# Two-layer encoder trunk on one core: weight sums by accumulating DMAs, and an instruction order from a timeline simulation

## The chip, the cores and the metric

One core of a Trainium2 chip runs the kernel: TensorE (PE) with its weight loads (PEld), VectorE (DVE), ScalarE (ACT), GpSimd (POOL) and SyncE (SP), whose queue issues nearly all DMAs. The metric is the time of one execution in microseconds (us).

## The reference

Two request batches, a prompt of 512 tokens and a sample of 256, go through two layers with shared weights (D = 1024, feed-forward width 2816). The kernel treats them as one block of 768 tokens.

```
x <- LN1(alpha*x + W_out [DiffAttn_ALiBi(x) ; BiMLSTM(x)])
x <- LN2(alpha*x + ConvGatedFFN(x))

s = einsum('bqhcd,bshcd->bhcqs', qi, k)           # 4 heads, 2 score maps each
p = softmax(s + bias, axis=-1)
a = p[:, :, 0] - lam * p[:, :, 1]
out = einsum('bhqs,bshd->bqhd', a, v)
```

Beside the four attention heads stand four heads of a two-directional mLSTM in chunks of 128 tokens. The feed-forward part multiplies by a gate matrix and an up matrix, runs a convolution of width 3 over the gate, and multiplies the result into the down matrix.

## The kernel before

**Arithmetic.** Each product is made in three matmul passes (PASSES) of operands split into a high part and a low part. `Weights` brings a weight piece of 128x512 in by an SP DMA (`_load`, six raw buffers, names raw0, raw1, ...) and converts it (`_conv`): ACT writes the high part wh (L171), DVE the low part wl (L172). Twelve slots hold converted pieces until PE has used them.

**Attention stage.** PE works through generators that `weave` mixes by fixed priorities. Per head, sequence and query block (the digits in a name: s2231 is head 2, sequence from token tile 2 on, block 3, map 1) the chain is: scores s on PE (L728, L729), tp on DVE (L730), two exponentials on ACT (L734), the difference of the maps in tp on DVE (L737), aT on PE (L740), a copy of aT, u on PE (L744), ao on DVE (L752, after a power on POOL), aoT on PE (L757). The mLSTM chunk c has qkT, kq and num on PE and pt, qet, den and hq on DVE (num20 is chunk 2, pair 0). Matmuls that depend on little stand between them as filling: lo (L345, one of the dense projections), and aqkA and aqkB (L355), the q and k projections of the next head, which DVE and ACT then split into sQ, sK and kL. Behind head 3 comes the output projection wo (L898).

**Feed-forward stage.** For each of 22 feature tiles of 128 per layer, `ff_tile` makes gate and up by a seven-product scheme (`product`, p1 to p7, L942) that needs four sums of weight pieces, T1 to T4. Two of them run on POOL and two on DVE (L149), on raw pieces, before conversion. After three tiles (four for one group) `down` runs 12 chunks dn (L1002), whose results DVE adds to acc (L1009). The pair of lines that makes a sum is in `Weights._value`.

**Order.** The program's instructions go to each engine in the order that the tile framework's scheduler gives them by their priorities. Each engine then runs its own list strictly in order.

Of the kernel before, what the change touches and what calls it, by code (L numbers as in the profile page):

```python
# [13 lines left out]
F32 = mybir.dt.float32  # L14
# [7 lines left out]
T = SA + SB  # L22
# [73 lines left out]
class Weights:  # L96

    def __init__(self, nc, raw_pool, hl_pool, prio):  # L100
        self.nc, self.raw_pool, self.hl_pool, self.prio = nc, raw_pool, hl_pool, prio
        self.dram, self.blocks = [], []
        self.uses, self.raw, self.hl = {}, {}, {}
        self.n_dma = self.n_conv = self.n_got = self.n_done = 0
        self.diff_pool = None
        self.urgency = PR_CONV

# [6 lines left out]

    def block(self, src, n, dst=None):
        self.blocks.append((src, n, dst))
        for j in self._pieces(src):
            self.uses[j] += 1
# [6 lines left out]
    def _pieces(self, src):  # L125

        if not isinstance(src, dict):
            return [src]
        if src.get("planned"):
            return []  # L130
        src["planned"] = True
        return self._pieces(src["a"]) + self._pieces(src["b"])


    def _load(self):

        while self.n_dma < len(self.dram) and (self.n_dma < NRAW or self.uses[self.n_dma - NRAW] == 0):
            ap, n = self.dram[self.n_dma]
            t = self.raw_pool.tile([128, WCOL], F32, tag="raw", name=f"raw{self.n_dma}")[:, :n]
            self.nc.sync.dma_start(t, ap)  # L140
            self.raw[self.n_dma] = t
            self.n_dma += 1

    def _value(self, src, n):
        if isinstance(src, dict):
            if "tile" not in src:
                a, b = self._value(src["a"], n), self._value(src["b"], n)
                src["tile"] = self.diff_pool.tile([128, 512], F32, tag=src["tag"], name=f"{src['tag']}_{self.n_conv}")
                src["engine"].tensor_tensor(out=src["tile"], in0=a, in1=b, op=ALU.subtract)  # L149
                for x in (src["a"], src["b"]):  # L150
                    if not isinstance(x, dict):
                        self.uses[x] -= 1
            return src["tile"]
        return self.raw[src]

    def _conv(self, i):
        src, n, dst = self.blocks[i]
        self._load()
        v = self._value(src, n)
        if callable(dst):  # L160
# [45 lines left out]
def trunk(ctx, nc, tc, d, o, depth=DEPTH):  # L206
# [59 lines left out]
    for l in range(depth):  # L266
        if l:
            for u in range(4):
                W.unit(d["w_c1"][l, u], 1056)
        for u in range(4):  # L270
            W.unit(d["w_av"][l, u])
        for h in range(4):
            W.unit(d["w_aq"][l, h])
            W.unit(d["w_ak"][l, h])
            if h == 0 or h == (1 if L1 else 2):
                for u in range(4):
                    W.unit(d["w_lv" if h == 0 else "w_lo"][l, u])
        for hf in range(2):
            for u in range(4):
                W.unit(d["w_out"][l, hf, u])  # L280
        early = {}
        for i in range(FF_EARLY):
            early[i] = [W.piece(d["w_g"][l, i, :, p * 512:(p + 1) * 512], 512) for p in range(2)]
            for src in early[i]:
                W.block(src, 512)
        for kind, i in ffn_seq:
            if kind == "f":

                def half(w, p):
                    return W.piece(d[w][l, i, :, p * 512:(p + 1) * 512], 512)  # L290

                if i in early:
                    g0, g1 = early[i]
                else:
                    g0, g1 = half("w_g", 0), None
                u0, u1 = half("w_u", 0), half("w_u", 1)
                if g1 is None:
                    g1 = half("w_g", 1)
                t1 = {"a": u0, "b": g0, "tag": "T1", "engine": G}
                t2 = {"a": u1, "b": t1, "tag": "T2", "engine": V}  # L300
                t3 = {"a": u1, "b": u0, "tag": "T3", "engine": G}
                t4 = {"a": t2, "b": g1, "tag": "T4", "engine": V}
# [65 lines left out]
    for l in range(depth):  # L368
# [502 lines left out]
        def combine(t):  # L871

            y0, y1 = acc[:, t, 0:512], acc[:, t, 512:1024]
            if t < 3:
                todo[t] = [(A11, y0), (A12, y1)]
                return
            x0, x1 = acc[:, t - 3, 0:512], acc[:, t - 3, 512:1024]
            E = V if t in VT else G
            s1, s2, s3, s4 = (sp.tile([128, 512], F32, tag=f"S{i}", name=f"S{i}_{t}") for i in (1, 2, 3, 4))
            E.tensor_tensor(out=s1, in0=y0, in1=y1, op=ALU.add)  # L880
            E.tensor_tensor(out=s2, in0=s1, in1=x0, op=ALU.subtract)
            E.tensor_tensor(out=s3, in0=x0, in1=y0, op=ALU.subtract)
# [62 lines left out]
        def ff_tile(f):  # L945
# [21 lines left out]
            V.scalar_tensor_tensor(out=g[:, hi_], in0=p4, scalar=-1.0, in1=u3, op0=ALU.mult, op1=ALU.add)  # L967
            p5 = bank(f"p5_{f}")
            product(p5, S1)
            V.tensor_tensor(out=u4, in0=p5, in1=u2, op=ALU.add)  # L970
            V.tensor_tensor(out=up[:, hi_], in0=p5, in1=u3, op=ALU.add)
# [128 lines left out]
def build(arrays, depth=DEPTH):  # L1100
# [18 lines left out]
```

## Time and profile before

| | us |
|---|---|
| median of three runs (1812.57 to 1816.02) | 1815.83 |
| the profiled execution | 1814.85 |
| its span, first to last instruction | 1813.1 |
| PE busy | 1772.2 |
| DVE busy | 1348.4 |
| ACT busy | 774.3 |
| POOL busy | 244.4 |

Busy times are sums over instructions in which neighbours may overlap: the pitch from one start to the next is shorter than a duration. The granted TensorE clock was 0.998 of full speed on average.

### The profile page before, as it was taken

What the parts mean: (1) busy time and instruction counts of PE and PEld (TensorE: products, weight loads), DVE (VectorE), ACT (ScalarE), POOL (GpSimd) and SP (SyncE); (2) the same over time, 40 slices, a digit from 0 to 9 for tenths busy, and PEclk for the clock granted to TensorE, in tenths of its full rate; (3) what the DMA queues carried; (4) which work ended last, traced back from release to release, by engine and by line L of the source; (5) the groups of instructions that cost most, each with busy time, mean ns of one, the idle gap of its engine ahead of it and who ended that gap; (6) DMA issues with size and microseconds to landing.
All of it is one profiled execution on the core that took longest, in us unless ns stands there. A gap on an engine that the chain in (4) does not pass through costs nothing. (4 is left out here: it accounts for less than half of the span.)

```text
span 1813.1 us, 26263 instructions
## 1 busy us (share of the span) xinstructions
PE 1772.2 (98%) x9692; PEld 1575.5 (87%) x9692; DVE 1348.4 (74%) x2592; ACT 774.3 (43%) x1636; POOL 244.4 (13%) x266
## 2 busy tenths in 40 slices
PE   8999999999999999999999999999999999999998
PEld 8877887889889889899898778878899898898996
DVE  4546887599877787787955468876997787787778
ACT  4445667144334334344233556671453343343340
POOL 2001011141111111110110011101411110111102
PEclk9999999999999999999999999999999999999999
DMA  5312221303122122123232123122122221221211
GB/s 190 100 53 71 76 60 59 139 24 95 57 82 82 47 82 73 56 69 96 94 97 80 53 64 94 47 86 107 37 87 70 65 82 51 78 82 47 82 65 70
DMA packets 89232, 138.09 MB, mean 76 GB/s; under 512 B 7792, under 2 KB 33008, under 8 KB 89104
## 3 DMA queue, kind: packets, MB, share of 16 engines
q1 hardware_dynamic: 88384, 136.05, 23.7%
q8 instruction: 76, 1.25, 0.3%
q14 instruction: 52, 0.43, 0.1%
q10 hardware_dynamic: 720, 0.37, 0.1%
HBM read 130.00 MB, written 6.39 MB: 75 GB/s over the span
## 5 line engine op out<-in xcount | busy, mean ns | idle before, releaser
L942 PE MATMUL p<-actA,wh 128*128 128x384 f32 x1408 | 363.5, 338 | 3.2 <-DVE g L967 3.2
L171 ACT ACTIVATE wh<-raw 128x512 fp32r<-128x512 f32 (+1 forms) x348 | 215.8, 631 | 275.3 <-PE p L942 110.1
L172 DVE TENSOR_TENSOR wl<-raw,wh 128x512 fp32r<-128x512 f32 (+1 forms) x348 | 244.0, 712 | 62.2 <-ACT wh L171 61.7
L942 PE MATMUL p<-actB,wh 128*128 128x384 f32 x1056 | 270.1, 337 | 0.0
L942 PEld LDWEIGHTS p<-actA,wh 128*128 128x128 f32 x1408 | 254.7, 188 | 5.8 <-DVE g L967 3.8
L942 PE MATMUL p<-actA,wl 128*128 128x384 f32 x704 | 237.3, 337 | 0.0
L149 POOL TENSOR_TENSOR T<-raw,raw 128x512 f32<-128x512 f32 x88 | 120.3, 1370 | 837.4 <-DVE wl L172 483.9
L1002 PE MATMUL dn<-wh,actB 128*128 128x512 f32 x576 | 209.1, 396 | 1.4 <-DVE acc L1009 1.4
L171 ACT ACTIVATE wh<-T 128x512 fp32r<-128x512 f32 x176 | 108.5, 629 | 220.6 <-DVE acc L1009 105.3
L942 PEld LDWEIGHTS p<-actB,wh 128*128 128x128 f32 x1056 | 191.2, 188 | 0.0
L1002 PE MATMUL dn<-wh,ring 128*128 128x512 f32 x480 | 179.2, 397 | 1.6 <-DVE acc L1009 1.6
L942 PE MATMUL p<-actB,wl 128*128 128x384 f32 x528 | 177.2, 336 | 0.0
L1009 DVE TENSOR_TENSOR acc<-acc,dn 128x512 f32<-128x512 f32 x144 | 98.3, 683 | 72.2 <-PE dn L1002 72.0
L172 DVE TENSOR_TENSOR wl<-T,wh 128x512 fp32r<-128x512 f32 x176 | 129.8, 749 | 22.1 <-ACT wh L171 22.0
L1002 PEld LDWEIGHTS dn<-wh,actB 128*128 128x128 f32 x576 | 108.0, 188 | 30.3 <-DVE acc L1009 3.4
L942 PEld LDWEIGHTS p<-actA,wl 128*128 128x128 f32 x704 | 132.2, 188 | 0.1
L898 PE MATMUL wo<-wh,actB 128*128 128x512 f32 x384 | 122.9, 397 | 0.0
L1002 PE MATMUL dn<-wl,actB 128*128 128x512 f32 x288 | 113.2, 393 | 0.0
L1002 PEld LDWEIGHTS dn<-wh,ring 128*128 128x128 f32 x480 | 90.0, 188 | 24.6 <-DVE acc L1009 4.2
L942 PEld LDWEIGHTS p<-actB,wl 128*128 128x128 f32 x528 | 99.1, 188 | 0.0
L1002 PE MATMUL dn<-wl,ring 128*128 128x512 f32 x240 | 94.7, 395 | 0.0
L898 PEld LDWEIGHTS wo<-wh,actB 128*128 128x128 f32 x384 | 71.8, 188 | 16.2
(270 smaller groups left out, 3387.9 us busy)
## 6 DMA issues: line engine op xcount, KB each, us to landing
raw<-in_w_g_dram SPq DMA_DIRECT2D x88, 256.0 KB, 2.8
raw<-in_w_u_dram SPq DMA_DIRECT2D x88, 256.0 KB, 2.6
raw<-in_w_down_dram SPq DMA_DIRECT2D x88, 256.0 KB, 2.7
raw<-in_w_out_dram SPq DMA_DIRECT2D x32, 256.0 KB, 2.7
pt<-scr_m SPq DMA_DIRECT2D x12, 512.0 KB, 3.9
qet<-scr_e SPq DMA_DIRECT2D x12, 512.0 KB, 5.2
raw<-in_w_c_dram SPq DMA_DIRECT2D x16, 264.0 KB, 4.0
raw<-in_w_av_dram SPq DMA_DIRECT2D x16, 256.0 KB, 3.5
```

Of the source, the lines that this page charges most:

```text
L149: src["engine"].tensor_tensor(out=src["tile"], in0=a, in1=b, op=ALU.subtract)
L171: self.nc.scalar.activation(h, v, AF.Identity)
L172: self.nc.vector.tensor_tensor(out=l, in0=v, in1=h.bitcast(F32), op=ALU.subtract)
L898: PE.matmul(p, actB[:, k, a, t * 128:(t + 1) * 128], units[k][1 + b], start=n + i == 0, stop=n == 7 and i == 2)
L942: PE.matmul(ps, blk[1 + a][:, k * 128:(k + 1) * 128], x[:, k, b, :], start=k + i == 0, stop=k == 3 and i == 2)
L1002: PE.matmul(p, x, (wh_, wl_)[b], start=k + i == 0, stop=k == nf - 1 and i == 2)
L1009: V.tensor_tensor(out=z, in0=z, in1=p, op=ALU.add)
```

## The change

**Sums by DMA.** For the first three feature tiles of each layer (N_ENG) the four sums stay on POOL and DVE. From the fourth tile on (19 tiles in each layer) a sum is one SP load into a T tile and one accumulating DMA that POOL issues onto it: T1 from DRAM, T2 from T1's tile, T3 from DRAM, T4 from T2's tile. All T tiles share a ring of four buffers (NSUM). Signs are arranged so that each sum is an addition, so the seven products are used with other signs and come in another order. Per tile eight DMAs for sums and three raw loads (2.75 MB) take the place of four raw loads (1 MB), and two POOL and two DVE instructions per tile are gone.

**Order.** The context is made with `schedule_with_timeline_sim=True`; the lists of all engines come out in another order.

```diff
@@ class Weights
+        while self.diff_pool is not None and self.n_sum < len(self.sums) and (self.n_sum < NSUM or self.sums[self.n_sum - NSUM]["read"]):
+            s = self.sums[self.n_sum]
...
+            t = self._slot(s)
+            self.nc.sync.dma_start(t, s["a"])
+            self.nc.gpsimd.dma_start(t, s["b"]["tile"] if isinstance(s["b"], dict) else s["b"], accum_op=ALU.add)
...
+    def _slot(self, s):
+        s["tile"] = t = self.diff_pool.tile([128, 512], F32, tag="T", name=f"T{self.n_sum}", bufs=NSUM)
...
-                src["engine"].tensor_tensor(out=src["tile"], in0=a, in1=b, op=ALU.subtract)
+                src["engine"].tensor_tensor(out=self._slot(src), in0=v[0], in1=v[1], op=ALU.add)
@@ the list of weight blocks
+                if i < N_ENG:
...
+                    t1 = W.sum(l, u0, g0, G)
+                    t2 = W.sum(l, u1, t1, V)
...
+                    u1 = W.piece(at("w_u", 1), 512)
+                    t1 = W.sum(l, at("w_u", 0), at("w_g", 0))
+                    t2 = W.sum(l, at("w_u", 1), t1)
+                    t3 = W.sum(l, at("w_u", 1), at("w_u", 0))
+                    t4 = W.sum(l, at("w_g", 1), t2)
-                for src in (t4, t2, t3, t1, u1) if i in early else (g0, g1, t4, t2, t3, t1, u1):
+                for src in (t1, t2, t3, t4, u1) if i in early else (g0, g1, t1, t2, t3, t4, u1):
@@ ff_tile
-            p4 = bank(f"p4_{f}")
-            product(p4, A22)
+            p5 = bank(f"p5_{f}")
+            product(p5, S1)
...
-            V.tensor_tensor(out=u2, in0=p6, in1=m1, op=ALU.add)
+            V.tensor_tensor(out=u2, in0=m1, in1=p6, op=ALU.subtract)
+            V.tensor_tensor(out=u4, in0=p5, in1=u2, op=ALU.add)
...
-    with tile.TileContext(nc) as tc:
+    with tile.TileContext(nc, schedule_with_timeline_sim=True) as tc:
```

The order is shown at three places, all in layer 0; layer 1 has the same pattern. In the rows an x at the end counts repeats, the number behind an underscore marks a tile, and line numbers of the changed kernel are 15 to 23 higher (L187 there is L172 before, L750 is L728).

**Place 1, middle of the attention stage.** PE's list behind qkT3, the transposes for mLSTM chunk 3, in the kernel before:

```order
L592 MATMUL qkT3_2180<-ident_214,hq_226 128x128 x4
L355 MATMUL aqkA21_2244<-actA_70,wh48_1456 128x512 x2
L355 MATMUL aqkA21_2244<-actA_70,wl48_1457 128x512
L728 MATMUL s2000_2353<-sK_229,sQ_228 128x256
L729 MATMUL s2000_2353<-kL_230,sQ_228 128x256
L728 MATMUL s2001_2357<-sK_229,sQ_228 128x256
L729 MATMUL s2001_2357<-kL_230,sQ_228 128x256
L345 MATMUL lo1_2478<-wh49_1462,actA_70 128x512
L345 MATMUL lo1_2478<-wl49_1463,actA_70 128x512
L345 MATMUL lo1_2478<-wh49_1462,actA_70 128x512
L345 MATMUL lo1_2478<-wh50_1468,actA_70 128x512
L345 MATMUL lo1_2478<-wl50_1469,actA_70 128x512
```

The list of PE there in the changed kernel, behind the same qkT3 and chunk 2's first products:

```order
L655 MATMUL num20_2189<-cst21_1804,qet2_2068 128x129
L658 MATMUL num20_2189<-vaug_237,pt2_2009 128x129 x2
L655 MATMUL num22_2317<-cst21_1804,qet2_2068 128x129
L658 MATMUL num22_2317<-vaug_237,pt2_2009 128x129 x2
L655 MATMUL num23_2318<-cst21_1804,qet2_2068 128x129
L658 MATMUL num23_2318<-vaug_237,pt2_2009 128x129 x2
L637 MATMUL kq3_2386<-qz_1847,kt3_2185 128x128 x4
L762 MATMUL aT200_2366<-ident_214,tp200_2350 128x128 x2
L766 MATMUL u20_2347<-av_227,aT200_2369 128x128 x2
L762 MATMUL aT201_2420<-ident_214,tp201_2404 128x128 x2
L614 MATMUL qkT4_2395<-ident_214,hq_226 128x128 x4
L750 MATMUL s2210_2590<-sK_229,sQ_228 128x512
```

The filling is gone from between. In the whole piece of the list from qkT3 to aoT22 the kernel before has 48 matmuls of lo (lo1 and lo2), 27 of aqkA and 38 of aqkB; the changed one has 24 (lo5). Those 113 now stand ahead of qkT3, and so do 72 more that stood behind aoT22 (lo3, lo4 and aqkA31).

DVE's list in the same piece, where chunk 4's den is made, before:

```order
L597 COPY qz_1847<-qkT5_2578 64x256
L730 ISA tp222_2665,mn222_2666<-s2220_2668,dneg_233 128x512
L730 ISA mn222_2666 128x1
L730 ISA tp222_2665,mn222_2666<-s2221_2672,dneg_233 128x512
L730 ISA mn222_2666 128x1
L643 SCALAR_TENSOR_TENSOR den40_2625<-num40_2615,cols_239 128x2
L643 SCALAR_TENSOR_TENSOR den41_2632<-num41_2616,cols_239 128x2
L644 TENSOR_TENSOR den40_2625<-num40_2615,den40_2625 128x2
L644 TENSOR_TENSOR den41_2632<-num41_2616,den41_2632 128x2
L645 RECIPROCAL den40_2625<-den40_2625 128x2
L682 SCALAR_TENSOR_TENSOR sg2_2718<-sgt2_2719,sg2_2718 128x512
L645 RECIPROCAL den41_2632<-den41_2632 128x2
```

And DVE's list in the changed kernel, behind the same den:

```order
L667 RECIPROCAL den41_2632<-den41_2632 128x2
L758 SCALAR_TENSOR_TENSOR cc223_2741<-sm022_2528,nlam_221,cc223_2741 128x1
L187 TENSOR_TENSOR wl65_3318<-raw65_2297,wh65_3317 128x512
L759 SCALAR_TENSOR_TENSOR tp223_2739<-tp223_2739,cc223_2741 128x512
L770 SCALAR_TENSOR_TENSOR sm022_2528<-sm022_2528 128x4
L187 TENSOR_TENSOR wl66_3324<-raw66_2303,wh66_3323 128x512
L187 TENSOR_TENSOR wl67_3330<-raw67_3297,wh67_3329 128x512
L670 SCALAR_TENSOR_TENSOR hq_226<-num40_2615,den40_2625,hq_226 128x128
L670 SCALAR_TENSOR_TENSOR hq_226<-num41_2616,den41_2632,hq_226 128x128
L187 TENSOR_TENSOR wl68_3336<-raw68_3303,wh68_3335 128x512
L187 TENSOR_TENSOR wl69_3342<-raw69_3309,wh69_3341 128x512
L704 SCALAR_TENSOR_TENSOR sg4_3201<-sgt4_3202,sg4_3201 128x512
```

Eight conversions of output weights, wl65 to wl72, have moved into this piece from behind head 3's first blocks; 256-wide pieces of aqkB3 have moved out of it. From the reading of qkT3 to ao22 the DVE list had 151 instructions (41 of 512 elements per partition, 16 of 256, 25 of 128, 69 of one to four) and has 150 (51, 8, 24, 67). SP's list in the piece also changes: the load of qet5, which DVE multiplies 12 rows further on, stands behind the raw loads 71 to 75, and raw75 uses the buffer of raw69.

**Place 2, end of the attention stage.** PE's list behind s3011, the last scores of head 3, before (lo5 goes on behind these rows for 19 more matmuls, with aoT32, u30 and aT301 between):

```order
L729 MATMUL s3011_3216<-kL_230,sQ_228 128x256
L345 MATMUL lo5_3253<-wh49_1462,actA_70 128x512
L345 MATMUL lo5_3253<-wl49_1463,actA_70 128x512
L744 MATMUL u32_2972<-av_227,aT323_3131 128x128 x4
L740 MATMUL aT300_3168<-ident_214,tp300_3152 128x128 x2
L345 MATMUL lo5_3253<-wh49_1462,actA_70 128x512
L345 MATMUL lo5_3253<-wh50_1468,actA_70 128x512
L345 MATMUL lo5_3253<-wl50_1469,actA_70 128x512
```

And in the changed kernel:

```order
L762 MATMUL aT323_3126<-ident_214,tp323_3110 128x128 x4
L766 MATMUL u32_2972<-av_227,aT323_3131 128x128 x4
L762 MATMUL aT300_3168<-ident_214,tp300_3152 128x128 x2
L762 MATMUL aT301_3225<-ident_214,tp301_3209 128x128 x2
L779 MATMUL aoT32_3143<-ident_214,ao32_3141 128x128 x4
L384 MATMUL loT5_3286<-ident_214,hq_226 128x128 x4
L766 MATMUL u30_3149<-av_227,aT300_3171 128x128 x2
L921 MATMUL wo02_3449<-wh64_3311,actB_2834 128x512
L921 MATMUL wo02_3449<-wl64_3312,actB_2834 128x512
L921 MATMUL wo02_3449<-wh64_3311,actB_2834 128x512
L766 MATMUL u30_3149<-av_227,aT301_3228 128x128 x2
L779 MATMUL aoT30_3249<-ident_214,ao30_3247 128x128 x2
```

The last scores are followed by their own transposes, the last u and the last aoT with 8 transposes and 3 matmuls of wo02 between; wo00's last three matmuls, which need the result of aoT30, come right behind, and most of wo00 and wo02 stand earlier.

**Place 3, the feed-forward stage.** PE's list at the first group of dn, before, at the passage from one chunk to the next (dn001 ends, dn002 begins):

```order
L1002 MATMUL dn001_4696<-wh106_4446,actB_2834 128x512
L1002 MATMUL dn001_4696<-wh107_4466,ring_4043 128x512
L1002 MATMUL dn001_4696<-wl107_4467,ring_4043 128x512
L1002 MATMUL dn001_4696<-wh107_4466,ring_4043 128x512
L1002 MATMUL dn002_4707<-wh105_4427,actB_2834 128x512
L1002 MATMUL dn002_4707<-wl105_4428,actB_2834 128x512
L1002 MATMUL dn002_4707<-wh105_4427,actB_2834 128x512
L1002 MATMUL dn002_4707<-wh106_4446,actB_2834 128x512
```

And in the changed kernel behind the same chunk:

```order
L1025 MATMUL dn001_4714<-wh107_4481,ring_4033 128x512
L1025 MATMUL dn001_4714<-wl107_4482,ring_4033 128x512
L1025 MATMUL dn001_4714<-wh107_4481,ring_4033 128x512
L965 MATMUL p1_4_4881<-actA_70,wh111_4580 128x384 x2
L965 MATMUL p1_4_4881<-actA_70,wl111_4581 128x384
L965 MATMUL p1_4_4881<-actA_70,wh111_4580 128x384 x2
```

Before, 12 chunks stand in a row; now products of the next feature tile come between pairs of chunks.

## Rows read from the trace of the kernel before

**Rows 1.** The page, part 1: busy us, share of the span and instructions.

```profile
PE 1772.2 (98%) x9692; PEld 1575.5 (87%) x9692; DVE 1348.4 (74%) x2592; ACT 774.3 (43%) x1636; POOL 244.4 (13%) x266
```

**Rows 2.** Windows: length, busy us (count) of PE, PEld, DVE, ACT, POOL, PEclk, DMA, GB/s.

```profile
104.40:217.00 112.60, 110.17 (x668) 89.85 (x667) 70.77 (x201) 61.42 (x178) 10.47 (x14) 1.00 0.19 57
217.00:270.10 53.10, 50.63 (x336) 44.40 (x335) 46.97 (x157) 38.78 (x126) 6.35 (x8) 1.00 0.22 65
270.10:329.90 59.80, 57.15 (x304) 46.50 (x303) 40.74 (x101) 37.07 (x95) 5.71 (x6) 1.00 0.33 118
1117.70:1171.40 53.70, 50.88 (x336) 44.15 (x335) 47.12 (x157) 38.57 (x125) 5.83 (x8) 1.00 0.22 65
452.20:870.20 418.00, 416.40 (x2161) 384.96 (x2161) 324.19 (x528) 156.98 (x255) 45.49 (x34) 1.00 0.24 74
```

**Rows 3.** Timeline of PE, layer 0: start, duration, line, operands, count.

```profile
217.00 0.60 PE L592 MATMUL qkT<-ident,hq 128*128 128x128 f32 x4
...
270.11 0.60 PE L757 MATMUL aoT<-ident,ao 128*128 128x128 f32 x4
```

**Rows 4.** Windows with the tile lo alone: PE, PEld, ACT.

```profile
217.00:270.10 53.10, 12.83 (x48) 8.66 (x48) 2.36 (x4) 1.00 0.22 65
```

**Rows 5.** Windows with the tile aqkA alone: PE, PEld, DVE, ACT.

```profile
217.00:270.10 53.10, 7.96 (x28) 4.86 (x27) 2.75 (x4) 3.49 (x6) 1.00 0.22 65
```

**Rows 6.** Windows with the tile aqkB alone: PE, PEld, DVE, ACT.

```profile
217.00:270.10 53.10, 5.79 (x38) 4.88 (x38) 1.28 (x4) 0.76 (x2) 1.00 0.22 65
```

**Rows 7.** Chain of waits, layer 1: start us, us on the chain, engine, line, count.

```profile
1219.65 45.25 PE wo L898 x195
...
1294.45 0.60 DVE S L880
...
1353.64 25.15 PE dn L1002 x108
...
1448.48 44.09 PE p L942 x252
```

**Rows 8.** Timeline of DVE in the middle of the attention stage.

```profile
221.48 0.40 DVE L730 CUSTOM_DVE_ANT_0 tp<-s,dneg 128x256 f32<-128x256 f32 x1
...
221.81 0.16 DVE L645 RECIPROCAL den<-den 128x2 f32<-128x2 f32 x1
221.89 0.40 DVE L730 CUSTOM_DVE_ANT_0 tp<-s,dneg 128x256 f32<-128x256 f32 x1
...
222.59 0.61 DVE L648 SCALAR_TENSOR_TENSOR hq<-num,den,hq 128x128 f32<-128x128 f32 x2 [0.29 <-ACT hq L647]
```

**Rows 9.** Timeline, layer 0, head 3: end of scores to tp, end of u to aoT.

```profile
287.01 0.39 PE L729 MATMUL s<-kL,sQ 128*128 128x512 f32 x1
...
290.13 0.75 DVE L737 SCALAR_TENSOR_TENSOR tp<-tp,cc 128x512 f32<-128x512 f32 x1
...
310.94 0.63 PE L744 MATMUL u<-av,aT 128*128 128x128 f32 x4
...
314.39 0.41 PE L757 MATMUL aoT<-ident,ao 128*128 128x128 f32 x2 [0.27 <-DVE ao L752]
```

**Rows 10.** The page, part 5: an ACT group, busy us and mean ns.

```profile
L171 ACT ACTIVATE wh<-raw 128x512 fp32r<-128x512 f32 (+1 forms) x348 | 215.8, 631 | 275.3 <-PE p L942 110.1
```

**Rows 11.** Waits of PE in 452.2:870.2: us in total, times, longest us.

```profile
PE dn L1002 <- DVE acc L1009: 1.6, 5, 0.6
```

**Rows 12.** Groups of DVE in 452.2:870.2, one of the two sums.

```profile
L149 DVE TENSOR_TENSOR T<-raw,T 128x512 f32<-128x512 f32 x18 | 12.3, 684 | 8.5 <-POOL T L149 8.5
```

**Rows 13.** The page, part 6: issues, KB each, median us to landing.

```profile
raw<-in_w_g_dram SPq DMA_DIRECT2D x88, 256.0 KB, 2.8
...
qet<-scr_e SPq DMA_DIRECT2D x12, 512.0 KB, 5.2
```

**Rows 14.** Windows at the end of the span, columns as in rows 2.

```profile
1804.00:1808.00 4.00, 0.96 (x5) 0.43 (x3) 2.92 (x8) 0.54 (x1) 3.21 (x3) 0.91 0.05 17
1808.00:1813.00 5.00, 0.00 (x0) 0.00 (x0) 1.63 (x5) 0.51 (x1) 1.15 (x2) 0.50 0.54 196
```

More of the change, by code (lines that the diff above doesn't have):

```diff
@@ L86 @@
 NSG = 3
+NSUM = 4
+N_ENG = 3
 AT1 = 11
@@ L103, in __init__ @@
         self.uses, self.raw, self.hl = {}, {}, {}
-        self.n_dma = self.n_conv = self.n_got = self.n_done = 0
+        self.n_dma = self.n_conv = self.n_got = self.n_done = self.n_sum = 0
+        self.sums = []
         self.diff_pool = None
@@ L116, in block, with sum @@
         self.blocks.append((src, n, dst))
-        for j in self._pieces(src):
-            self.uses[j] += 1
+        for x in (src["a"], src["b"]) if isinstance(src, dict) and src["engine"] else (src,):
+            if not isinstance(x, dict):
+                self.uses[x] += 1
+    def sum(self, layer, a, b, engine=None):
+        s = {"a": a, "b": b, "engine": engine, "layer": layer, "read": False}
+        self.sums.append(s)
+        return s
     def unit(self, ap, n=1024):
@@ L142, in _load @@
             self.n_dma += 1
+        while self.diff_pool is not None and self.n_sum < len(self.sums) and (self.n_sum < NSUM or self.sums[self.n_sum - NSUM]["read"]):
+            s = self.sums[self.n_sum]
+            if s["layer"] != self.layer:
+                break
+            if s["engine"]:
+                break
+            t = self._slot(s)
[3 more added lines that the diff above has]
+        s["tile"] = t = self.diff_pool.tile([128, 512], F32, tag="T", name=f"T{self.n_sum}", bufs=NSUM)
+        self.n_sum += 1
+        return t
     def _value(self, src, n):
@@ L146, in _value @@
             if "tile" not in src:
-                a, b = self._value(src["a"], n), self._value(src["b"], n)
-                src["tile"] = self.diff_pool.tile([128, 512], F32, tag=src["tag"], name=f"{src['tag']}_{self.n_conv}")
-                src["engine"].tensor_tensor(out=src["tile"], in0=a, in1=b, op=ALU.subtract)
+                v = [x["tile"] if isinstance(x, dict) else self.raw[x] for x in (src["a"], src["b"])]
+                src["engine"].tensor_tensor(out=self._slot(src), in0=v[0], in1=v[1], op=ALU.add)
                 for x in (src["a"], src["b"]):
@@ L172, in _conv @@
         self.nc.vector.tensor_tensor(out=l, in0=v, in1=h.bitcast(F32), op=ALU.subtract)
-        if not isinstance(src, dict):
+        if isinstance(src, dict):
+            src["read"] = True
+        else:
             self.uses[src] -= 1
@@ L180, in pump @@
         while self.n_conv < len(self.blocks):
-            if isinstance(self.blocks[self.n_conv][0], dict) and self.diff_pool is None:
-                break
+            if isinstance(self.blocks[self.n_conv][0], dict):
+                self._load()
+                if self.diff_pool is None or ("tile" not in self.blocks[self.n_conv][0] and not self.blocks[self.n_conv][0]["engine"]):
+                    break
             if self.blocks[self.n_conv][2] is None:
@@ L287, in trunk, with at @@
             if kind == "f":
[L289 to L293, printed above, removed]
-                else:
[L295 to L302, printed above, removed]
-                for src in (t4, t2, t3, t1, u1) if i in early else (g0, g1, t4, t2, t3, t1, u1):
+                def at(w, p):
+                    return d[w][l, i, :, p * 512:(p + 1) * 512]
+                g0, g1 = early[i] if i in early else [W.piece(at("w_g", p), 512) for p in range(2)]
+                if i < N_ENG:
+                    u0, u1 = [W.piece(at("w_u", p), 512) for p in range(2)]
+                    t1 = W.sum(l, u0, g0, G)
+                    t2 = W.sum(l, u1, t1, V)
+                    t3 = W.sum(l, u1, u0, G)
+                    t4 = W.sum(l, g1, t2, V)
+                else:
+                    u1 = W.piece(at("w_u", 1), 512)
[4 more added lines that the diff above has]
+                for src in (t1, t2, t3, t4, u1) if i in early else (g0, g1, t1, t2, t3, t4, u1):
                     W.block(src, 512)
@@ L818, in trunk @@
         DF = ExitStack()
+        W.layer = l
         W.diff_pool = df = DF.enter_context(tc.tile_pool(name=f"df{l}", bufs=1, reuse_waits="tile"))
@@ L966, in ff_tile @@
             V.tensor_tensor(out=u3, in0=p7, in1=u2, op=ALU.add)
[L967 to L971, printed above, removed]
+            V.scalar_tensor_tensor(out=up[:, hi_], in0=p5, scalar=-1.0, in1=u3, op0=ALU.mult, op1=ALU.subtract)
+            p4 = bank(f"p4_{f}")
+            product(p4, A22)
+            V.tensor_tensor(out=g[:, hi_], in0=p4, in1=u3, op=ALU.add)
             p3 = bank(f"p3_{f}")
             product(p3, S4)
-            V.tensor_tensor(out=up[:, lo_], in0=p3, in1=u4, op=ALU.add)
+            V.scalar_tensor_tensor(out=up[:, lo_], in0=p3, scalar=-1.0, in1=u4, op0=ALU.mult, op1=ALU.subtract)
             S.activation(c, g, AF.Identity, bias=cb, scale=w1)
```

13 lines of the change are left out of this document (3 added, 10 removed).

## The prediction

> **What bounds the kernel now.** I read the shares of the engines first, then the attention stage in windows, then the waits and the pitch of single instructions. PE is busy for 1772.2 of 1813.1 us [rows 1], so only some 41 us are there to be won. Two kinds of stretch must be told apart [rows 2]. In the feed-forward stage PE works 416.40 of 418.00 us; DVE has 94 us of slack, DMA is at 0.24, and nothing that lightens DVE, POOL or SP there can shorten it by more than 1.6 us a layer. In the attention stage PE is busy 110.17 of 112.60, then 50.63 of 53.10, then 57.15 of 59.80 us. In the second of these three DVE is busy for 46.97 of 53.10: both engines are nearly full at once, and layer 1 repeats it (50.88 and 47.12 of 53.70). There each engine's order decides.
>
> **The sums (part 1 of the change).** Of 22 tiles per layer, 19 lose two POOL and two DVE sums. On DVE that is 76 instructions for both layers; the row shows 684 ns each [rows 12], 0.60 at the pitch of such instructions [rows 7], so 46 us of DVE. It is cover, not path: PE's only named wait in the window is 1.6 us for acc [rows 11], and a T is made long before PE takes it. I count nothing. If that cover were gone, the gain could not exceed the 1.6.
>
> What comes instead is off the path too. Per tile SP issues four more loads, and POOL issues four accumulating DMAs. POOL runs in order: T2 reads T1's tile and T4 reads T2's, so each of these two has to wait for an earlier one to land; the tile costs POOL's queue about 2a, with a the time of one accumulate. A tile takes PE 418.0/18 = 23.2 us on average [rows 2], so POOL keeps up as long as a is below 11.6. No accumulate is in this trace. From below, a plain load of the same 256 KB lands in 2.8 us, and one of 512 KB in 5.2 [rows 13]. From above three such loads (read, read, write) and one POOL instruction of a sum (45.49/34 = 1.3 [rows 2]) make 9.7. I take 5, nearest to the 512 KB row, since an accumulate has to read its target as well as its source. Both ends are harmless: 0 us. The bytes go from 1 to 2.75 MB a tile; if DMA's 0.24 grows with them, it reaches about 0.6, still not full.
>
> **The order (part 2), middle of the attention stage.** The markers are the starts of qkT3 and aoT22, at 217.00 and 270.11 [rows 3], 53.1 us apart. Between them stood 48 matmuls of lo [rows 4], 27 of the 28 of aqkA that the window counts, since one began before the marker [rows 5], and 38 of aqkB [rows 6]. At 45.25/195 = 0.232 us for one of 512 columns [rows 7], and half of it for one of 256, the change takes out 24 net of lo, 27 of aqkA and 38 of aqkB: 5.6 + 6.3 + 4.4 = 16.3 us. Some 0.9 us of other matmuls come in. If PE still set the length, the stretch would now last 53.1 - 15.4 = 37.7 us, and the 15.4 would be spent ahead of it.
>
> But DVE's list there is not shorter. Prices at the pitch: 0.60 for 512 elements [rows 7], 0.38 for 256 (the next start follows after 0.33, the next of its kind after 0.41, with a small one between), 0.26 for 128 (two of them in 0.61), 0.08 for the small ones (221.81 to 221.89) [rows 8]. Before: 41 x 0.60 + 16 x 0.38 + 25 x 0.26 + 69 x 0.08 = 42.7 us. After: 51 x 0.60 + 8 x 0.38 + 24 x 0.26 + 67 x 0.08 = 45.2 us. DVE takes its inputs from PE and gives PE its next ones (tp, pt, qet, hq), two buffers deep, so it can't do this list much ahead. PE therefore has 37.7 us of work and DVE at least 45.2. That is the lower end: +7.5. The upper end keeps DVE's share of waiting as it was: 45.2 x 53.1/42.7 = 56.2, or +18.5. I take DVE's busy time of before, changed by the list: 46.97 + 10 x 0.60 - 8 x 0.38 - 0.26 = 49.7, so **+12.0 per layer**. It is nearer to the lower end, since DVE rather than PE now ends the waits. What is late next is qet5: its load stands on SP behind raw75, which needs raw69's buffer, free after wl69. From wl69 to the use of qet5 stand about 3.3 us of DVE's list, and the load takes 5.2 [rows 13]; those 2 us are inside the 49.7.
>
> **End of the attention stage.** PE now has, between the last score of s3011 and aT301, ten small transposes and products, at most 1.6 us (four of them take 0.63 [rows 9]). Before, the step from the last score to a finished tp took from 287.40 to 290.88, 3.5 us [rows 9]: PE waits 1.9. Behind the last u nothing stands before aoT30; this step took from 311.57 to 314.39, 2.8 us [rows 9]. Behind aoT30 wo00 needs two ACT passes of some 0.63 [rows 10], 1.3. Together 6.0 us of waiting against 2.65 of idle time in that window before [rows 2], so **+3.4 per layer**. The lower end is 0, if the waits that were there before are all that is left. The upper end is +10: the window also lost 96 matmuls of lo and aqkA, 96 x 0.232 = 22 us, so PE holds 57.15 - 22 = 35 us of work there, and DVE, without the eight conversions and two of kL at 0.68, 40.74 - 6.8 = 34, with no cover for the waits of either.
>
> **Start of the attention stage.** The 185 matmuls now stand here, and transposes follow their scores at a greater distance. PE's idle time in it is 112.60 - 110.17 = 2.4 us [rows 2]; I let all of it go: **-2.4 per layer**, at least 0.
>
> **Feed-forward stage.** Chunks of dn stood 12 in a row, each waiting for DVE to empty a bank; now products stand between. The 1.6 us of wait [rows 11] go: **-1.6 per layer**. p and dn themselves keep their pitch (44.09/252 and 25.15/108 us [rows 7]); the other order of the seven products changes which result is last, and DVE has the slack for it.
>
> **Sum.** Per layer 12.0 + 3.4 - 2.4 - 1.6 = 11.4; both layers +22.8. On the profiled execution of before, 1814.85 (1.75 above its span, 0.98 below the median of the three runs), that is 1837.65, rounded to 1838. With all lower bounds: 7.5 + 0 - 2.4 - 1.6 = 3.5, twice 7.0, 1822. With all upper bounds: 18.5 + 10 + 0 + 0, twice 57, 1872; all at once is unlikely. The likeliest case's own range is 1822 to 1866.
>
> **Rivals.**
> *Faster.* DVE reaches qkT3 with part of its list already done, so the stretch follows PE. It decides when DVE is more than 8.0 us ahead in each layer (the 12.0 less the 4.0 that the start and the feed-forward stage give back) and the end costs nothing. For it speaks that DVE is busy only 70.77 of 112.60 us in the stretch before [rows 2], against it the two buffers. With all 12.0 ahead, the idle time of the first two stretches goes (2.4 + 2.5 per layer) and the 1.6 of the feed-forward stage: 1814.85 - 13 = 1802, or 1806 with some of the late waits left.
> *Same.* DVE is ahead by just those 8.0 us, 12.0 - 8.0 - 4.0 = 0: 1815.
> *Clock.* TensorE falls to the lower of its two levels in the starved stretch. At the end of the span, with PE at 0.00 of 5.00 us, the granted clock is 0.50, and with PE at 0.96 of 4.00 it is 0.91 [rows 14]; all windows where PE is busy 95% show 1.00 [rows 2]. Here PE would be at 37.7 of 49.7, 76%, between these rows and with gaps of a few us at most, so I hold it unlikely. If it happened throughout, the 50.63 - 16.3 + 0.9 = 35.2 us of matmuls would take 70.4, which is 20.7 over DVE's 49.7: 1838 + 41 = 1879, and half as much over, 1858, if for half of the time. The Trainium skill, "TensorE: Matmul & The Clock Gate", Part 1, says that an idle array is put to 1.2 GHz and that gaps between bursts of matmuls bring it there in the middle of a kernel; the row at 0.50 agrees, and no run here shows it for gaps of this size.
> *Slow accumulates.* If a is over 11.6, POOL's queue sets the pace of the feed-forward stage: 38 tiles x (2a - 23.2), at a = 12.5 that is 68 us, 1880 or more. Against it stand 2.8 and 5.2 [rows 13]. The Trainium skill, "DMA: Bandwidth & Descriptors", Anatomy of one DMA, fits a DMA issued from GpSimd as 2.0 us plus its bytes at 436 GB/s; for 256 KB that is an estimate of 2.6 us, by which this rival would be out. It is a fit for copies, and no run here shows an accumulate.
>
> **How the numbers follow.** A measurement tells 0.2%, 3.6 us, from no change. Chances: forecast 0.55, faster 0.17, same 0.12, clock 0.09, slow accumulates 0.07. Slower is 0.55 + 0.09 + 0.07 = 0.71. The range may leave out 2 in 10: below 1806 lies about half of the faster case (0.09), above 1868 lie the slow accumulates (0.07) and about half of the clock case (0.04). So it runs from 1806 to 1868.
>
> **What would show it.** Right: between the same two markers about 50 us instead of 53.1 with PE busy under 40, waits of PE for DVE (tp, pt, den, hq) of some 12 us in each layer; the windows before s3011's end with 1 to 3 us waits of aT and aoT; dn without its wait; POOL's accumulates done well before wh is made of them. Wrong: a stretch near 38 us with PE full; PE waiting in the feed-forward stage for p, or wh waiting for T; a granted clock under 1.00 there. The weakest step is how far DVE can run ahead into the stretch.

## The result and the profile after

The changed kernel takes 1914.95 us (median of four runs), the kernel before 1814.95 beside it: 1.0554 times as long, with an interval of 1.0536 to 1.0573. The forecast was 1838 and the range ended at 1868. The direction was right, the size was not: 100 us instead of 23. The page of the changed kernel, part 1 and TensorE's clock in 40 slices, against [rows 1]:

```profile
PE 1804.7 (94%) x9692; PEld 1613.1 (84%) x9692; DVE 1291.5 (68%) x2516; ACT 779.9 (41%) x1636; POOL 265.8 (14%) x342
```

```profile
PEclk9999988998999999999999999889899999999999
```

PE is busy 32.5 us longer for the same 9692 matmuls, and idle 67.4 us longer (1913.0 - 1804.7 = 108.3, against 40.9). The clock row says where it was lowest: in slices 6, 7 and 10 and again in 26, 27 and 29, which are the same places of the two layers. The windows that answer to [rows 2] (same columns: length, busy us of PE, PEld, DVE, ACT, POOL, granted clock, DMA share, GB/s) stand here for both layers, and with them, as the fourth and the seventh row, the passage from wo to the feed-forward stage. The markers are those of the prediction: qkT3 begins at 253.68, aoT22 at 317.91.

```profile
104.60:253.70 149.10, 148.12 (x870) 125.78 (x869) 85.23 (x236) 78.09 (x215) 9.69 (x14) 1.00 0.17 54
253.70:317.90 64.20, 46.14 (x247) 38.53 (x246) 48.38 (x152) 39.79 (x125) 5.30 (x8) 0.81 0.24 74
317.90:368.40 50.50, 37.95 (x190) 30.51 (x190) 25.40 (x68) 20.36 (x60) 5.10 (x6) 0.86 0.07 22
...
416.00:475.50 59.50, 47.53 (x251) 43.57 (x250) 51.06 (x72) 26.90 (x45) 17.66 (x16) 0.86 0.31 82
1201.60:1267.60 66.00, 45.69 (x247) 37.37 (x246) 49.77 (x154) 40.58 (x126) 5.36 (x8) 0.84 0.24 72
1267.60:1317.80 50.20, 37.44 (x190) 30.12 (x190) 25.31 (x68) 20.29 (x60) 5.11 (x6) 0.90 0.06 24
...
1365.50:1424.70 59.20, 47.43 (x251) 43.49 (x250) 50.84 (x72) 26.85 (x46) 17.56 (x16) 0.86 0.31 83
504.90:919.70 414.80, 414.80 (x2162) 386.06 (x2161) 287.31 (x487) 155.24 (x253) 58.61 (x67) 1.00 0.59 146
```

The same passage in the kernel before, from the start of the last chunk of wo to that of the third feature tile:

```profile
377.40:422.80 45.40, 43.04 (x252) 39.49 (x251) 43.76 (x67) 23.97 (x43) 13.38 (x12) 1.00 0.15 47
```

Set side by side, layer 0 / layer 1, in us:

| stretch | before | after | difference |
|---|---|---|---|
| s0000 to qkT3 | 112.6 / 112.9 | 149.1 / 149.0 | +36.5 / +36.1 |
| qkT3 to aoT22 | 53.1 / 53.7 | 64.2 / 66.0 | +11.1 / +12.3 |
| aoT22 to wo03 | 59.8 / 59.9 | 50.5 / 50.2 | -9.3 / -9.7 |
| last chunk of wo to third feature tile | 45.4 / 45.2 | 59.5 / 59.2 | +14.1 / +14.0 |
| dn000 to dn600 | 418.0 / 417.6 | 414.8 / 415.1 | -3.2 / -2.5 |

The first three lines belong together. The 185 matmuls that moved ahead of qkT3, and ten more of aqkB3 from behind aoT22 that I had not counted, are worth 147 x 0.232 + 48 x 0.116 = 39.7 us, and the three stretches together got longer by 38.3 (layer 1: 38.7). So before, this work filled time in which PE would otherwise have waited (the run f1 below tests this); now it takes its full time in the first stretch, and the two stretches that it left got no shorter: together they are 1.8 us longer (layer 1: 2.6).

What PE waits for in the middle stretch (line, waited for, us in total, times, longest):

```profile
PE kq L637 <- DVE hq L670: 3.3, 3, 2.4
PE num L655 <- DVE qz L619: 2.9, 2, 2.4
PE aT L762 <- DVE hq L670: 2.9, 1, 2.9
PE u L766 <- ACT aT L764: 1.9, 3, 0.7
...
```

And DVE in the same stretch:

```profile
DVE qet L644 <- DMA qet<-scr_e: 5.0, 3, 3.4
DVE den L665 <- PE num L658: 3.7, 5, 1.5
DVE hq L670 <- ACT hq L669: 2.5, 5, 0.7
DVE qz L618 <- ACT kt L617: 2.1, 1, 2.1
```

No single wait makes up the difference. PE waits for what DVE makes (hq, qz, aT), and DVE waits for what PE, ACT and the DMA of qet make: the two take turns.

The feed-forward stage went as forecast: PE is busy for all of its 414.80 us, and the accumulating DMAs are in time. Their landing times, and POOL's part of the work for each (0.87 us of POOL, a share of the 58.61 us above):

```profile
T<-T POOLq DMA_DIRECT2D x76, 256.0 KB, 3.8
...
T<-in_w_g_dram POOLq DMA_DIRECT2D x38, 256.0 KB, 4.5
...
T<-in_w_u_dram POOLq DMA_DIRECT2D x38, 256.0 KB, 5.5
```

```profile
L153 POOL DMA_DIRECT2D T<-T x34 | 29.6, 871 | 116.2 <-DMA T<-T 26.5 <-DVE c L1000 21.7 <-DVE wl L187 17.1
```

### The profile page after: what moved, and what is told of

The parts are those of the page before. It is cut to its first block, busy times and chain, and to the rows that moved or that the text cites. A ratio compares the mean times of both kernels' runs of the same rounds, so it can differ in the third digit from the quotient of the medians.

```text
span 1913.0 us, 26812 instructions
## 1 busy us (share of the span) xinstructions
PE 1804.7 (94%) x9692; PEld 1613.1 (84%) x9692; DVE 1291.5 (68%) x2516; ACT 779.9 (41%) x1636; POOL 265.8 (14%) x342
## 5 line engine op out<-in xcount | busy, mean ns | idle before, releaser
L187 DVE TENSOR_TENSOR wl<-raw,wh 128x512 fp32r<-128x512 f32 (+1 forms) x348 | 238.2, 691 | 71.1 <-ACT wh L186 70.7
L965 PEld LDWEIGHTS p<-actA,wh 128*128 128x128 f32 x1408 | 259.6, 190 | 7.9 <-ACT actA L386 1.6
L921 PE MATMUL wo<-wh,actB 128*128 128x512 f32 x384 | 128.8, 412 | 9.2 <-ACT actB L386 6.2
L187 DVE TENSOR_TENSOR wl<-T,wh 128x512 fp32r<-128x512 f32 x176 | 123.7, 722 | 0.0
L153 POOL DMA_DIRECT2D T<-T x76 | 66.1, 870 | 263.1 <-DMA T<-T 40.6
L153 POOL DMA_DIRECT2D T<-in_w_g_dram x38 | 33.5, 881 | 474.0 <-DMA T<-in_w_u_dram 181.5
```

The source lines that it names most:

```text
L153: self.nc.gpsimd.dma_start(t, s["b"]["tile"] if isinstance(s["b"], dict) else s["b"], accum_op=ALU.add)
L921: PE.matmul(p, actB[:, k, a, t * 128:(t + 1) * 128], units[k][1 + b], start=n + i == 0, stop=n == 7 and i == 2)
L965: PE.matmul(ps, blk[1 + a][:, k * 128:(k + 1) * 128], x[:, k, b, :], start=k + i == 0, stop=k == 3 and i == 2)
```

## The experiments

### The two halves of the change apart

```diff
 e1_old_order: the changed kernel
-    with tile.TileContext(nc, schedule_with_timeline_sim=True) as tc:
+    with tile.TileContext(nc) as tc:
 e2_order_only: the kernel before
-    with tile.TileContext(nc) as tc:
+    with tile.TileContext(nc, schedule_with_timeline_sim=True) as tc:
```

In the attention stage the first has PE's list of before, the second that of the changed kernel (their traces show the same rows of PE there).

> The changed kernel's sums by DMA with the order of instructions of before (attention stage: the same list on PE). Theory O, the order costs all of the 100 us and the sums cost nothing: 1811 to 1817 us, granted clock 1.00, attention stage from s0000 to wo03 225.5 us as before. Theory D, the accumulating DMAs cost part of it: 1830 or more, with waits of p or of wh for T in the feed-forward stage.

> The kernel before with the new order alone; sums stay on POOL and DVE. Theory O: 1905 to 1918 us, the middle stretch qkT3 to aoT22 64 us at a granted clock of 0.81, and waits between wo and p1 as in the changed kernel. Theory D: under 1880.

Measured: e1 1819.72 us, ratio 1.0029 (1.0018 to 1.0040); e2 1907.19 us, ratio 1.0510 (1.0492 to 1.0528). Of the 100 us the order alone brings 93. In the order of before, the sums cost 5, a little more than theory O's upper end of 1817 and far less than theory D's 1830; beside the new order they cost 7.8 (1914.95 - 1907.19). The middle and the last stretch of e2, and its passage to the feed-forward stage:

```profile
253.60:317.90 64.30, 43.49 (x248) 35.54 (x247) 48.33 (x153) 39.68 (x124) 5.35 (x8) 0.89 0.24 74
317.90:370.10 52.20, 39.05 (x191) 31.21 (x191) 25.43 (x69) 20.32 (x60) 5.10 (x6) 0.84 0.08 26
417.60:473.50 55.90, 47.38 (x251) 44.13 (x250) 50.47 (x75) 26.48 (x45) 18.29 (x14) 0.88 0.17 57
```

The middle stretch is as long as with the sums by DMA (64.3 against 64.2; in layer 1 it is 64.4 against 66.0), at a clock of 0.89 where 0.81 was expected. The passage takes 55.9 us against 59.5 (layer 1: 56.0 against 59.2): most of what the sums cost beside the new order lies here, 3.4 us per layer. Theory O holds for the order; that the sums cost nothing was not met.

In e1 the 5 us lie in two places of the trace: 4.4 us in layer 0 and 1.8 in layer 1 around the first tile whose sums come by DMA, and 3.8 in layer 0 where num waits for qet. A shorter dn000 to dn600 (415.0 us and 416.7 instead of 418.0 and 417.6) makes up for a part. The first place, ACT's waits there:

```profile
ACT wh L186 <- DMA T<-T: 10.8, 4, 7.5
```

So a third kernel, the old order with the sums by DMA from the seventh tile on:

```diff
-N_ENG = 3
+N_ENG = 6
```

> Sums by DMA in the order of before, but only from the seventh feature tile on (N_ENG 6) instead of the fourth. If the 5.3 us of the old order with DMA sums are the first such tile coming late, once a layer: 1808 to 1815. If every tile by DMA costs a little: 1817 to 1820.

Measured: 1813.28 us, ratio 0.9996 (0.9987 to 1.0005): the 5 us are not a price of each tile. In the trace of this kernel num does not wait for qet in layer 0, and neither of the waits for up (L991), 2.8 and 1.5 us at e1's first such tile, is there. Why qet came late in e1 alone was not tried. In the old order and from the seventh tile on, the sums by DMA are neither a gain nor a loss that can be measured, although dn000 to dn600 takes 416.3 us instead of 418.0.

### Is it the missing filling?

```diff
 f1_thin: the kernel before
     def tok_major(t, blocks, ps, cols, thin=False):
+        if thin:
+            PE.matmul(ps, xh(0, t, 0), blocks[0][1][:, cols], start=True, stop=True)
+            return
...
-                tok_major(t, units, p, slice(0, 512))
+                tok_major(t, units, p, slice(0, 512), tag == "lo" and t > 0)
...
-                feat_major(uu, pA, pBu)
+                feat_major(uu, pA, pBu, (0, 1) if h == 3 else ())
```

> The kernel before, in its own order, with lo1 to lo5 and head 3's aqkA and aqkB cut from 24 matmuls to one each (this leaves out 42.7 us of TensorE's work per layer, and the results are not those of the reference). The stretch from qkT3 to wo03, 112.9 us before, loses its filling as in the changed kernel. Theory F, the waits of the two engines for each other are there in either order and the filling only covered them: the stretch keeps at least 95 us and the run 1778 or more. Theory T, it is the new order's short distances between an instruction and the one that needs it: the stretch falls to 75 to 85 us, the run to 1735 to 1758.

Measured: 1796.18 us, ratio 0.9900 (0.9883 to 0.9916). Leaving out 85 us of matmuls won 18. The two stretches of both layers:

```profile
219.60:280.10 60.50, 42.74 (x233) 35.45 (x232) 48.64 (x161) 44.34 (x138) 5.86 (x8) 0.83 0.18 57
1113.20:1172.90 59.70, 42.97 (x234) 35.69 (x233) 48.72 (x160) 44.40 (x138) 5.84 (x8) 0.83 0.19 58
280.10:322.10 42.00, 35.62 (x194) 28.27 (x192) 31.99 (x88) 25.88 (x73) 5.81 (x6) 0.92 0.18 59
1172.90:1214.10 41.20, 34.81 (x195) 27.47 (x193) 31.94 (x89) 25.63 (x73) 5.81 (x6) 0.96 0.18 61
```

They take 102.5 us (100.9 in layer 1), where they took 112.9 (113.6). The middle stretch even got longer than it was with the filling, 60.5 against 53.1 [rows 2], with four instructions more on DVE and the clock at 0.83. Theory F holds: without the filling, 60.5 of the 64.2 us come under the old scheduler too. One reserve: the scheduler made its lists anew, and in the trace scores, kq and num follow each other in a somewhat different order than before, so the filling is not all that differs. In the last stretch it is different: 42.0 here, 50.5 in the changed kernel.

### What the length of DVE's list is worth

```diff
 g2_poolwl: the changed kernel
+POOL_WL = (*range(65, 73), *range(327, 335))
...
-        self.nc.vector.tensor_tensor(out=l, in0=v, in1=h.bitcast(F32), op=ALU.subtract)
+        (self.nc.gpsimd if i in POOL_WL else self.nc.vector).tensor_tensor(out=l, in0=v, in1=h.bitcast(F32), op=ALU.subtract)
```

> The changed kernel with the eight conversions that had moved into the middle stretch (wl65 to wl72, and those of layer 1) made on POOL instead of DVE; the order of everything else is nearly the same. DVE's list in the stretch loses 8 x 0.60 = 4.8 us. Theory D (that of the prediction), the length of DVE's list sets the stretch: 64.2 falls by 4.8 or more, to 59 or less, in each layer, the run by 10, to 1905. Theory P, PE and DVE wait for each other in turn and the list's length matters little: the stretch stays at 62 to 65 and the run at 1909 to 1916.

Measured: 1903.18 us, ratio 1.0489 (1.0473 to 1.0504), 11.8 us less than the changed kernel. The middle stretches:

```profile
252.90:313.00 60.10, 43.72 (x254) 35.28 (x253) 47.09 (x148) 40.61 (x127) 16.72 (x16) 0.91 0.26 79
1196.90:1258.50 61.60, 43.38 (x253) 35.08 (x252) 48.09 (x149) 41.16 (x129) 16.74 (x16) 0.92 0.26 77
```

The stretch fell by 4.1 and 4.4 us, to 60.1 and 61.6: a little less than theory D asked for (59 or less), while theory P would have had it stay at 62 or more. The run fell by 11.8, where D had 10 and P at most 6. But DVE's busy time fell by only 1.3 us (48.38 to 47.09; layer 1: 1.7). While POOL converts, instructions of DVE beside it take longer:

```profile
293.45 10.93 POOL L188 TENSOR_TENSOR wl<-raw,wh 128x512 fp32r<-128x512 f32 x8 [12.24 <-ACT wh L187]
```

```profile
293.46 1.83 DVE L760 SCALAR_TENSOR_TENSOR tp<-tp,cc 128x512 f32<-128x512 f32 x1
295.22 1.25 DVE L771 SCALAR_TENSOR_TENSOR sm<-sm 128x4 f32<-128x4 f32 x1
```

In the changed kernel such a tp takes 0.74 us and this sm 0.16. The other 2.8 us of the 4.1 are shorter waits of DVE: 3.1 us in total for qet instead of 5.0, and none for aT instead of 1.2. So it is shown that work taken off DVE's list shortens the stretch, and that 13 to 16 us of waits stand beside that list, not the 4.5 that I had allowed (49.7 less 45.2); it is not shown that the length of the list alone does it.

### What the clock is worth

```diff
 e4_scores3 (e5_scores2 with range(2 ...)): the changed kernel
-                        PE.matmul(ps[:, :n], sQ[:, c, qtok], sK[:, c, keys], start=True, stop=False)
-                        PE.matmul(ps[:, :n], sQ[:, c, qtok], kL[:, c, keys], start=False, stop=True)
+                        for _ in range(3 if h > 1 else 1):
+                            PE.matmul(ps[:, :n], sQ[:, c, qtok], sK[:, c, keys], start=True, stop=False)
+                            PE.matmul(ps[:, :n], sQ[:, c, qtok], kL[:, c, keys], start=False, stop=True)
```

> The changed kernel with each pair of score matmuls of heads 2 and 3 issued three times, so that PE has about 12.7 us more to do in each middle stretch (33 us become 46), at the places where it waits. Theory C, the fall of TensorE's clock is what made the stretch 64 us instead of 50: the clock stays near 1.00 there and the stretch gets shorter in spite of the added work, 52 to 60 us, the whole run at most 1905. Theory W, waits for DVE's list alone make the 64 us and the clock costs little: the stretch stays at 64 or grows toward 77, the whole run 1913 to 1960.

> The changed kernel with each pair of score matmuls of heads 2 and 3 issued twice (three times gave 61.5 and 62.4 us for the middle stretch at a clock of 0.97, with 12.7 us more work; once gives 64.2 and 66.0 at 0.81 and 0.84). Theory C, the clock costs some us that the added work gives back: clock 0.9 or more and a stretch of 59 to 62, at 6 us more work. If the gain at three times came from a chance of the order: 64 to 67.

Measured: e4 1915.35 us, ratio 1.0559 (1.0543 to 1.0574); e5 1915.84 us, ratio 1.0564 (1.0547 to 1.0582). The middle stretches, three times first, then twice:

```profile
255.00:316.50 61.50, 50.87 (x303) 42.89 (x302) 49.59 (x155) 39.68 (x122) 5.74 (x8) 0.97 0.26 78
1203.30:1265.70 62.40, 50.84 (x302) 42.80 (x301) 49.57 (x155) 39.55 (x122) 5.74 (x8) 0.97 0.25 76
```

```profile
255.50:316.30 60.80, 45.35 (x281) 36.96 (x280) 48.70 (x155) 40.46 (x126) 5.31 (x8) 1.00 0.25 79
1200.80:1264.60 63.80, 47.25 (x281) 38.32 (x280) 48.80 (x155) 40.40 (x126) 5.31 (x8) 0.97 0.25 75
```

The clock came back to between 0.97 and 1.00, and the stretches got shorter by 2.2 to 3.6 us (64.2 and 66.0 in the changed kernel), though PE had 6 or 13 us more to do in them. Neither theory of e4 was met whole: the clock is C's and the run W's, since other stretches lost what this one won, and 61.5 us lie between C's 60 and W's 64. e5 met theory C in layer 0 (60.8) and missed it in layer 1 (63.8). What follows is a size. Between twice and three times PE has 6.4 us more to do, and the stretch changes by +0.7 and -1.4: this added work costs nearly nothing. So the 2 to 4 us are about what the clock costs in this stretch, if the first doubling too costs nothing, and not the 14 that lie between 49.7 and 64.

There is a rival for a part of these: DVE's wait for qet, 5.0 us in each layer of the changed kernel, is 1.3 and 2.2 in e4. In e5 it is 3.9 and 5.8, so there it explains at most 1.1 us of the gain in layer 0 and none in layer 1. In the changed kernel PE is busy in the stretch for 46.14 us; e5 has 45.35 at the full clock with 6.4 us of added matmuls in it, some 39 without. So the lower clock makes the matmuls about 7 us longer (an estimate from these rows); 2 to 4 of them show in the length of the stretch, and the rest takes the place of waiting. For the other stretches this was not tried.

### The passage to the feed-forward stage

I had no term for it. In the trace of the changed kernel PE stands for 6.7 us at one place there, and DVE's list shows what it does meanwhile (start, duration, idle before):

```profile
421.43 1.04 PE L384 MATMUL y0T<-ident,S 128*128 128x128 f32 x8
...
429.44 1.12 PE L384 MATMUL y0T<-ident,S 128*128 128x128 f32 x4 [6.74 <-POOL S L905]
```

```profile
419.01 1.28 DVE L874 SCALAR_TENSOR_TENSOR acc<-acc,mva,lng 128x1024 f32<-128x1024 f32 x1
420.21 3.57 DVE L187 TENSOR_TENSOR wl<-T,wh 128x512 fp32r<-128x512 f32 x4
423.70 2.28 DVE L880 SCALAR_TENSOR_TENSOR acc<-acc,rsa,lnb 128x1024 f32<-128x1024 f32 x1
425.91 0.68 DVE L187 TENSOR_TENSOR wl<-raw,wh 128x512 fp32r<-128x512 f32 x1
426.51 1.75 DVE L164 TENSOR_TENSOR T<-raw,T 128x512 f32<-128x512 f32 x1
428.18 1.75 DVE L187 TENSOR_TENSOR wl<-T,wh 128x512 fp32r<-128x512 f32 x1
```

Between the first half of the layer norm of a token tile (L874) and its second half (L880) stand four conversions, and behind it three more instructions for weights; POOL, which has to make S from the result, begins at 426. Two of these take 1.75 us each, while POOL makes S from 426.07 to 429.38; a conversion or sum with no such work of POOL beside it takes 0.69 (the median of 512 in this trace). Counted in DVE's rows of the traces, layer 0, from the reading of wo10 to that of the last transposed piece of the normed tokens: 5 conversions before; 12 conversions and 4 sums, 16 together, in the changed kernel; 13 and 4, 17 together, in e2. The expectation of the next run counts the sums in the 5 and the 16, but not in its 13 and 12. The converse, in the order of before:

```diff
 c_conv100: the kernel before
-PR_CONV1 = -100
+PR_CONV1 = 100
```

> The kernel before with one number changed, which puts 12 conversions and sums of feed-forward weights on DVE ahead of the last pieces of the layer norm instead of 5 (the new order has 16, with engine sums 13). Theory L, these instructions ahead of the norm are what the new order's 14 us per layer between wo and the fourth feature tile come from: 8 to 12 us per layer, 1830 to 1838. Rival: that loss is only a late consequence of the starved stretch ahead of it, and here the time is 1812 to 1818.

Measured: 1840.08 us, ratio 1.0145 (1.0130 to 1.0160), 26 us more, which is a little over the expected end of 1838. The stretch from the last chunk of wo to the fourth feature tile, first in the kernel before, then here for both layers:

```profile
377.40:437.50 60.10, 57.74 (x336) 54.19 (x335) 58.42 (x92) 30.59 (x54) 15.98 (x14) 1.00 0.17 53
```

```profile
376.10:449.30 73.20, 63.44 (x336) 58.48 (x334) 63.15 (x99) 34.74 (x57) 17.85 (x15) 0.88 0.18 58
1290.50:1361.90 71.40, 61.20 (x335) 55.98 (x334) 62.98 (x99) 34.70 (x57) 17.49 (x15) 0.93 0.19 60
```

Before, it took 60.1 us, and 59.9 in layer 1: +13.1 and +11.5. In the trace 16 conversions and sums (12 and 4) stand on DVE in the piece counted above, 11 more than before and as many as in the changed kernel, so one costs about 1.1 us. Theory L holds in this: such a loss needs no starved stretch ahead of it. That the changed kernel's 14 us are all of this kind is not shown. What share of the loss is the lower clock (0.88 and 0.93; PE is busy 5.7 us longer in layer 0 for as many matmuls), and what share the order of p and the transposes y0T on PE, which the number shifted too, was not tried apart.

### An attempt to beat both kernels

```diff
 un_m300: u_neng6
-PR_CONV1 = -100
+PR_CONV1 = -300
```

> An attempt to beat both kernels: the order of before, sums by DMA from the seventh feature tile on (1813.3 before this, against 1814.0), and one number changed so that four instead of five conversions and sums stand on DVE ahead of the last pieces of the layer norm. If a conversion ahead of the norm costs 1 to 2 us a layer, as the other way round showed (7 more cost 12 us a layer): 1809 to 1812. If the few that are left there are covered: 1812 to 1815.

Measured: 1812.80 us, ratio 0.9996 (0.9987 to 1.0005): no difference, as the second case of the expectation has it. (The 7 in the first leaves out the four sums; with them it is 11.) Nothing that was tried beats the kernel before.

## Why the prediction was right and wrong

**The sums, 0 us: right for a tile in the middle of the feed-forward stage, too low for the whole change.** One accumulate landed in 3.8 to 5.5 us, where I took 5, no p waits from dn000 to dn600, and DMA's share there is 0.59, where I took 0.6. That POOL is busy 0.87 us for each was not forecast; 58.61 us of POOL there against 45.49 [rows 2] cost nothing. What I missed is the first such tile of a layer, which comes late in the order of before (e1), and 3.4 us per layer in the passage beside the new order: the sums cost 7.8 us of the 100.

**Start of the attention stage, -2.4: right** (36.5 - 39.7 = -3.2), though PE's idle time there fell only from 2.4 to 1.0 us; the rest is that its busy time grew by 38.0 us and not by 39.7.

**Feed-forward stage, -1.6: right in sign, too small** (-3.2 and -2.5). Its explanation was not needed: e1 has no products between the chunks of dn, and takes 415.0 us as well (416.7 in layer 1).

**Middle of the attention stage, +12.0: the step that failed in size.** Against 37.7 us it is +26.5, and the stretch is 64.2 long, beyond the upper end of 56.2. DVE's busy time was nearly right (48.4, forecast 49.7), and so was that work taken off DVE shortens the stretch (g2). Wrong was "It is nearer to the lower end, since DVE rather than PE now ends the waits". With the filling gone DVE waits too, for num, for qet's DMA, for ACT: 15.8 us of 64.2, against 6.1 of 53.1 [rows 2]. The late qet5, which I had put at 2 us and inside the 49.7, belongs to these waits: DVE waits 5.0 us for qet in all, 3.4 of them for this one. f1 shows that most of the loss comes with the missing filling under the old scheduler too; the clock adds some 2 to 4.

**End of the attention stage, +3.4: too small, +14.2** (50.5 against 59.8 - 22.3 - 1.2 = 36.3). The three waits that I priced at 6.0 together are there and smaller: 1.1 for aT301, 2.0 for the last aoT, 1.0 for wo. But the window begins with idle time that I had left out, wo's first matmuls waiting for the last pieces of the mLSTM part (3.1), and it runs at 0.86:

```profile
317.90:332.00 14.10, 9.27 (x44) 7.30 (x45) 10.36 (x26) 7.71 (x23) 3.17 (x4) 0.76 0.01 1
332.00:350.00 18.00, 18.00 (x103) 15.48 (x102) 7.82 (x24) 6.80 (x20) 0.00 (x0) 1.00 0.00 0
350.00:368.40 18.40, 10.68 (x47) 7.74 (x45) 7.23 (x19) 5.85 (x19) 1.93 (x2) 0.81 0.18 60
```

PE is idle for 4.8 us in the first part and 7.7 in the last. f1, with the old order and without filling, takes 42.0: so some 5.7 us come with the missing filling and 8.5 with the new order and the clock. How these two share the 8.5 was not tried. The prediction's upper end of +10 for this stretch, and the 1866 that ends the likeliest case's range, have no sum behind them.

**The passage, no term: the step that is missing.** It makes +14 per layer. In e2, with the order alone, it is +10.5. Of the 14.1 us in layer 0, PE is idle for 9.6 more and busy for 4.5 more at the lower clock (47.53 us against 43.04, for 251 matmuls and 252). Together the terms are now -3.2 + 26.5 + 14.2 - 3.2 + 14.1 = 48.4 per layer, close to half of the 100.

**The rival on the clock**, given 0.09, was right that the clock falls in the starved stretches, and wrong by far on what that costs in the middle stretch. The rows of one fall in e1 show how it goes. PE had been idle since 442.65; then (start, duration):

```profile
442.31 0.34 PE L965 MATMUL p<-actA,wl 128*128 128x384 f32 x1
445.45 1.01 PE L965 MATMUL p<-actA,wh 128*128 128x384 f32 x2 [2.79 <-DVE up L991]
...
446.57 0.84 PE L965 MATMUL p<-actA,wh 128*128 128x384 f32 x2
...
448.43 0.51 PE L965 MATMUL p<-actA,wh 128*128 128x384 f32 x2
```

Two matmuls of 384 columns take 0.84 to 1.01 us where they took 0.51, and three us later 0.51 again. In the middle stretch of the changed kernel the same happens behind waits of 2.4 and 1.5 us. The Trainium skill, "TensorE: Matmul & The Clock Gate", Part 1, which says that gaps between bursts of matmuls bring the lower clock, is borne out in kind by these rows. What the lower clock costs is told by e4 and e5, and for the middle stretch alone. The other three rivals did not come.

## What to carry to other kernels

Where two in-order engines are both nearly full, count independent work that stands between dependent instructions as cover, and price its removal by what the stretch takes without it: here 39.7 us of matmuls moved ahead, and the two stretches that they left gave nothing back. When a scheduler makes a new order, look through every passage between stages, and count how many instructions of another chain now stand on the busiest engine ahead of the one that the next stage waits for; eleven conversions and sums ahead of a layer norm cost about as much (13.1 and 11.5 us in c_conv100) as the middle of the attention stage was forecast to (12.0).

## What the runs showed of the hardware that was not expected

An accumulating DMA of 256 KB that POOL issues lands in 3.8 us from SBUF to SBUF and in 4.5 to 5.5 from DRAM, against 2.8 for a plain load, and costs POOL 0.87 us. TensorE's clock fell to half, the lower of its two levels, behind idle times of 2.3 and 2.8 us in an otherwise full stretch (e1, at 215 and at 445: granted 0.57 from 216 to 220 and 0.50 from 446 to 448). Instructions of DVE took up to 1.83 us instead of 0.74 while POOL worked beside them (g2), and a conversion 1.75 instead of 0.69 (the changed kernel's passage). And the middle stretch was shorter with work added on PE (e4, e5), as it was longer with work taken away (f1).
